# A two-layer trunk on one core: which adaLN vectors TensorE makes around the norms, and which VectorE makes as rows

## The chip, the cores and the metric

The kernel runs on one core of a Trainium2 chip. The metric is the device time of one execution in microseconds (us); lower is better. The core has TensorE (PE; the load of its weights is listed apart as PEld), VectorE (DVE), ScalarE (ACT), GpSimd (POOL) and a queue for transfers (SP), each with its own stream of instructions, which wait for each other by semaphores.

## What is computed

Two layers, each a token mixer and a channel mixer (FFN), on x of 256 tokens by 1024 channels. Each layer first makes six vectors of 1024 from the condition c (adaLN), and each norm is scaled and shifted by two of them:

```python
c_act = jax.nn.silu(c)
for l in range(DEPTH):
    mod = c_act @ w_mod[l] + b_mod[l]
    sh1, sc1, g1, sh2, sc2, g2 = jnp.split(mod, 6, axis=-1)
    h = modulate(rms_norm(x, mix_norm_g[l]), sh1, sc1)
    y = token_mixer(h, ...)          # latent attention, block attention, gated convolution, w_out
    x = x + g1[:, None, :] * y
    h = modulate(rms_norm(x, ffn_norm_g[l]), sh2, sc2)
    x = x + g2[:, None, :] * channel_mixer(h, ...)   # w_up, depthwise conv, silu(a) * b, w_down
```

`modulate(n, sh, sc)` is n * (1 + sc) + sh. So a norm's scale (sc1, sc2) is wanted as soon as that norm's statistics are there; the shift at the same time; the gates g1 and g2 at the end of the mixer and of the FFN.

## The kernel before

x stays on the chip, transposed: eight tiles of 128 channels by 256 tokens. Every matrix is streamed from memory in units of 512 KB. Each matmul is exact to fp32 by three passes: a unit is loaded (line 193), ACT rounds it to a high part `whi` (line 210), DVE takes the difference `wlo` (line 212), and PE multiplies high by high (line 287), low by high (288) and high by low (290); lines 281 to 283 are the same three for a whole flush. All units go through one queue in the order in which the code asks for them.

An adaLN vector of layer l, number r (0 to 5 for sh1, sc1, g1, sh2, sc2, g2), lies in `mod[l]` as eight columns of 128. There are two ways to make one. As **rows** (`mod_row`, lines 369 to 373): for each k of eight a unit of the transposed matrix is loaded (`in_wmr`), DVE multiplies it by silu(c), which stands in every partition (`crow`), and sums along the row (line 367), and adds the bias (368); PE has no share in it. As a **PE part** (`mod_part`, lines 375 to 398): for each k a unit of `in_wm` is loaded and four matmuls with silu(c) as weights take it (line 384); after eight such steps ACT copies the sum (389), PE turns it by two transposes (392), and DVE adds the bias (394). A part is a generator: whoever calls `step` decides where its steps fall in the program.

Before, the twelve vectors are made so: as rows (0,0) and (0,1) in front of the first norm, (0,3) and (0,4) in layer 0's mixer, (1,0) and (1,1) in layer 0's FFN (`rows_left`), (1,2) in layer 1's mixer; as PE parts (0,2) in layer 0's mixer, (0,5) around layer 0's second norm, (1,3) around layer 1's first, (1,4) in layer 1's mixer (among its attention), (1,5) around layer 1's second norm.

A norm inside the program is `norm_stats(fill)`. First two steps (F1) of the part `fill` are taken. Squares (ACT line 475, DVE 483) are summed over channels by PE (487), DVE and POOL make the reciprocal root (465, 466), PE spreads it over the partitions (495), and the other six steps follow the statistics. Then `norm_tile` makes each of the eight tiles: DVE multiplies x by gain and root (528), ACT makes the high part (529), DVE the low one (530). The gain (1 + sc) * g comes from `mod_gain` (536). The part that ran here feeds a vector that is used later; its copy and transposes are taken after the second block of FFN matmuls (`step(fill)` at j == 1), or after the first matmuls of the mixer.

The work in the mixers is put in order by a planner (`STEPS`, `_order`), and a list scheduler then sets the order on each engine; what the code writes late may so stand early on its engine. The lines that the change touches are those of `mod_part`, `norm_stats` and `layer`.

Of the kernel before, what the change touches and what calls it, by code (L numbers as in the profile page):

```python
# [9 lines left out]
F32 = mybir.dt.float32  # L10
# [7 lines left out]
P = 128  # L18
S = 256
NB = 2  # L20
# [14 lines left out]
PB = 4  # L35
DVN = ()
MAHEAD = 0
F1 = 2
MARK = 1
CROWB = 1  # L40
C0K = {}
# [3 lines left out]
HOLD = 0  # L45
SQ4 = 1
CHAIN = 1
RPARTS = [(0, 3), (0, 4), (1, 2)]
RFROM = ("G", 5, 0)
RTO = ("PR", 5)  # L50
MFROM = ("QKV", 2, 0)
# [4 lines left out]
LEAD = 16  # L56
TAILP = 2
FLEAD = 1
ROWS = [(0, 0), (0, 1), (1, 0), (1, 1)] + RPARTS


PARTS = [[(0, r) for r in (2, 3, 4) if (0, r) not in RPARTS], [(1, 4)]]


UNITS = {"KL": 0.65, "QKV": 1, "UQ": 2, "UK": 2, "MA": 0.6, "BA": 0.7, "C": 1, "G": 1, "O": 1, "OC": 0.5, "PR": 1}
# [82 lines left out]
def trunk_kernel(ctx, tc, xT, crow, ccol, pos, invf, modb_d, cols_d, grow_d, wmr, wm, win1, wqkv,  # L148
# [223 lines left out]

        return use_row(wload_row(l, r, k, tag), row, l, r, k, scale)

    def mod_part(l, r, spare=True):

        acc = psa()
        raws = []
        for k in range(KD):
            for i in range(len(raws), min(KD, k + 1 + MAHEAD)):  # L380
                raws.append(wload(wm[l, r, i], SPARE[i % 4], 1) if spare else wload(wm[l, r, i]))
            raw = raws[k]
            for c in range(4):
                te.matmul(acc[32 * c:32 * c + 32, 0:S], cact[:, k:k + 1].to_broadcast([P, 32]),  # L384
                          raw[:, c * S:(c + 1) * S], start=(k == 0), stop=(k == KD - 1),
                          tile_position=(0, 32 * c))
            yield
        g = e1()
        ac.activation(g, acc[:, 0:S], AF.Copy)
        pt = psa()  # L390
        for q in range(2):
            te.transpose(pt[:, q * P:(q + 1) * P], g[:, q * P:(q + 1) * P], ident)
        view = pt[:, 0:S].rearrange("p (q c m) -> p c q m", q=2, c=4)[:, :, :, 0]
        ve.tensor_tensor(mod[l][:, r * 8:r * 8 + 8].rearrange("p (c q) -> p c q", c=4), view,
                         modb[:, l, r * 8:r * 8 + 8].rearrange("p (c q) -> p c q", c=4),
                         op=ALU.add)
        yield
# [5 lines left out]
    def step(gen, n=1):  # L403
        for _ in range(n):
            next(gen, None)
# [257 lines left out]
    def layer(l):  # L663

        sh1 = mod[l][:, 0:8]
        fill = mod_part(1, 3) if l == 1 else None
        hh, hl = new_h()
        if l == 0:

            bc = first_stats(crow0[1])  # L670
            xn = [mq().rearrange("p (k t) -> p k t", k=4) for _ in range(2)]

            bcs = e1()
            ac.activation(bcs, bc, AF.Copy)
            for k in range(KD):
                (gp if XNP and k else ve).tensor_tensor(xn[k // 4][:, k % 4, :], x[:, k, :], bcs, op=ALU.mult)
            mods0, gains = [], []

            def prepare_tile(k):
                raws0 = [wload_row(0, r, k) for r in range(2)]  # L680
                if k == 0:
                    load_rest()
                accs = small(2, "m0", 4)
                for r in range(2):
                    ve.scalar_tensor_tensor(raws0[r], raws0[r], 1.0, crow0[0], op0=ALU.mult, op1=ALU.mult,
                                            accum_out=accs[:, r:r + 1])
                mods0.append(ve.tensor_tensor(mod[0][:, 0:16].rearrange("p (r k) -> p k r", r=2)[:, k, :], accs,
                                              modb[:, 0, 0:16].rearrange("p (r k) -> p k r", r=2)[:, k, :], op=ALU.add))
                g = small(1, "gs", 12)
                i = ve.scalar_tensor_tensor(g, mod[0][:, 8 + k:9 + k], 1.0, cv(l, "mix_g")[:, k:k + 1],  # L690
                                            op0=ALU.add, op1=ALU.mult)
                gains.append(g)
                if HOLD:
                    hold[0] = i.ins

            prepare_tile(0)
        else:
            bc = norm_stats(fill)
        if l == 1:
            gs1 = mod_gain(l, 1, "mix_g")  # L700

        def rows(pp, w, k, b, start, stop):
# [48 lines left out]
        for k in range(KD):  # L751
            if l > 0:
                norm_tile(k, bc, gs1[:, k:k + 1], sh1[:, k:k + 1], hh, hl)
                conv_in(k)
                continue
            t = e1()
            ac.activation(t, xn[k // 4][:, k % 4, :], AF.Identity, scale=gains[k], bias=sh1[:, k:k + 1])
            ac.activation(hh[:, k, :], t, AF.Copy)  # L758
            last = ve.tensor_tensor(hl[:, k, :], t, hh[:, k, :].bitcast(F32), op=ALU.subtract)
            if HOLD > 1:  # L760
                hold[0] = last.ins
            latents(k)
            if k + 1 < KD:
                prepare_tile(k + 1)
            else:
                with tc.issue_after(mods0[-1].ins):
                    make_trig()
            conv_in(k)
            if k in C0K:
                gate_c(0, C0K[k], 3, psa)  # L770
            hold[0] = None
        step(fill or iter(()))
        ahead[0] = AHEAD
        mods = mod_parts(*((*p, False) for p in PARTS[l]))

        if l == 0:
            make_bases()
# [47 lines left out]


        qks = [None, None]
        vb = wk.tile([P, NB, 512], F32, tag="vb", name=nm("vb"), bufs=1)

        pqkv = {}  # L830

# [166 lines left out]

        def conv(j, t0, t1):
            if not cacc:  # L1000
                cacc.append(wk.tile([P, 4, S], F32, tag="lh2", name=nm("cacc"), bufs=1))
            aj = cacc[0][:, j, :]
            for t in range(t0, t1):
                if t == 0:
                    ve.tensor_scalar(aj, upad[:, j, 0:S], cw[:, j * 31:j * 31 + 1], cv(l, "cdw_b")[:, j:j + 1],
                                     op0=ALU.mult, op1=ALU.add)
                else:
                    ve.scalar_tensor_tensor(aj, upad[:, j, t:t + S], cw[:, j * 31 + t:j * 31 + t + 1], aj,  # L1008
                                            op0=ALU.mult, op1=ALU.add)
# [130 lines left out]
                                    x[:, n, :], op0=ALU.mult, op1=ALU.add)  # L1140


        gs2 = mod_gain(l, 4, "ffn_g")
        fill = mod_part(l, 5)
        bc = norm_stats(fill)
        hh, hl = new_h()
        marks = [norm_tile(k, bc, gs2[:, k:k + 1], mod[l][:, 24 + k:25 + k], hh, hl) for k in range(KD)]
        fw = wk.tile([P, 3, 44], F32, tag="fw", name=nm("fw"), bufs=1)
# [6 lines left out]
            ve.tensor_scalar(fb[:, NF:44], cv(l, "fdw_b")[:, NF:44], 0.5, None, op0=ALU.mult)  # L1155
        acc2 = []
        acts = []
        rows_left = [(1, r, k) for r in range(2) for k in range(KD)] if l == 0 else []

        def down(j):  # L1160
            if not acc2:
# [6 lines left out]
                flush(j == NF - 1)  # L1168

        hi_tags[:] = [("whi", 4), ("mq", 3)]  # L1170
        lo_tags[:] = [("wlo", 4), ("qkT", 2), ("wlo", 4), ("kv", 2)] if l else [("wlo", 4), ("qkT", 2), ("wlo", 4), ("kv", 2), ("wlo", 4), ("qkT", 2), ("wlo", 4), ("thc", 1)]
        def up(j):
            pp = psb()
            for _ in range(2):
# [29 lines left out]
        for is_up, j in FFN:  # L1204
            if not is_up:
                down(j)
                continue
            with ExitStack() as es:
                if j < 2:
                    for i in marks[MARK]:  # L1210
                        es.enter_context(tc.issue_after(i.ins))
                up(j)
            if j == 1:
                step(fill)
        hi_tags[:] = [("whi", 4)]
        lo_tags[:] = [("wlo", 4)]
        for n in range(KD):
# [92 lines left out]
```

## Time and profile before

| | |
|---|---|
| median of 3 runs | 938.41 us (935.89 to 938.76) |
| profiled execution | 933.22 us, of which span 931.3 us |
| mean granted clock of PE | 0.983 |
| PE busy | 897.1 us (96%) |
| DVE busy | 793.5 us (85%) |
| ACT busy | 554.0 us (59%) |
| POOL busy | 45.8 us (5%) |
| DMA | 201.59 MB, mean 216 GB/s |
| loads of rows / of PE parts | 56 / 40, 512 KB each |

Busy times count the time in which an engine has work in it. PE's records overlap, and its ends are modelled, so a PE busy in 100% of a stretch can still be faster or slower there: how many matmuls it took says that. A timeline row may join several instructions of one kind (xcount). A number in brackets behind a row is the time in which the engine stood before it, with what released it. In the rows an fp32 matmul of the parts and of the statistics has two records.

### The profile page before, as it was taken

How to read it: one execution, taken by the hardware profiler on the slowest of the kernel's cores; microseconds unless marked ns; L12 is line 12 of the kernel's file. 1: busy time of each engine (PE TensorE's matmuls, PEld its weight loads, DVE VectorE, ACT ScalarE, POOL GpSimd, SP SyncE). 2: the span in 40 equal slices, each digit the busy share in tenths (PEclk: the TensorE clock that was granted, in tenths of full speed). 3: DMA queues.
4: the chain of work that ended last, by engine and by line, in shares of the span. 5: the costliest groups of instructions: out<-in, count | busy, mean ns of one | idle time of the engine just before them, and what ended most of it. 6: DMA issues, size and time to landing. Idle time of an engine off the chain costs nothing.

```text
span 931.3 us, 18548 instructions
## 1 busy us (share of the span) xinstructions
PE 897.1 (96%) x7262; PEld 844.8 (91%) x7262; DVE 793.5 (85%) x1540; ACT 554.0 (59%) x979; POOL 45.8 (5%) x32
## 2 busy tenths in 40 slices
PE   3999999999989999999999999999999999999997
PEld 3998878998987999999979987889999799999997
DVE  5999899999987999988865999999787788777774
ACT  4577688744645655566643775895475566555551
POOL 1011500000000000000000042000000000000000
PEclk7999999999999999999999999999999999999999
DMA  7956524497886888877644565547657677555641
GB/s 282 397 206 209 178 92 155 158 325 274 298 307 234 290 273 286 304 239 224 214 137 129 184 231 184 195 130 270 230 180 259 211 234 223 186 184 187 187 127 46
DMA packets 58264, 201.59 MB, mean 216 GB/s; under 512 B 6976, under 2 KB 8512, under 8 KB 58176
## 3 DMA queue, kind: packets, MB, share of 16 engines
q1 hardware_dynamic: 58176, 200.41, 64.0%
q8 instruction: 57, 0.93, 0.4%
q14 instruction: 31, 0.25, 0.1%
HBM read 199.33 MB, written 1.05 MB: 215 GB/s over the span
## 4 chain that ended last, share of the span: by engine, by line
PE 80%; DVE 10%; DMA 4%; issue 2%; ACT 2%; POOL 2%; SPq 0%; POOLq 0%; DVEq 0%; ACTq 0%
PE psb L287 16%; PE psb L288 15%; PE psb L290 15%; PE psa L287 8%; PE psa L288 8%; PE psa L290 8%; DVE wlo L212 3%; DMA raw<-in_wmr 3%; DVE cacc L1008 2%; PE psa L384 2%; POOL rs L466 2%; PE psa L621 1%; DVE raw L367 1%; PE psa L281 1%; PE psa L633 1%
## 5 line engine op out<-in xcount | busy, mean ns | idle before, releaser
L210 ACT ACTIVATE whi<-raw 128x1024 fp32r<-128x1024 f32 (+2 forms) x286 | 294.6, 1038 | 212.1 <-PE psb L288 101.6
L212 DVE TENSOR_TENSOR wlo<-raw,whi 128x1024 fp32r<-128x1024 f32 (+2 forms) x286 | 340.5, 1195 | 74.0 <-ACT whi L210 62.7
L287 PE MATMUL psb<-hh,whi 128*128 128x256 f32 x1088 | 263.0, 282 | 1.6 <-ACT thc L729 1.2
L288 PE MATMUL psb<-hl,whi 128*128 128x256 f32 x1088 | 260.8, 280 | 0.0
L287 PEld LDWEIGHTS psb<-hh,whi 128*128 128x128 f32 x1088 | 205.0, 189 | 8.6 <-issue 5.3
L288 PEld LDWEIGHTS psb<-hl,whi 128*128 128x128 f32 x1088 | 205.3, 189 | 1.1 <-DVE e L528 0.4
L290 PE MATMUL psb<-hh,wlo 128*128 128x256 f32 x1088 | 149.8, 279 | 0.0
L290 PEld LDWEIGHTS psb<-hh,wlo 128*128 128x128 f32 x1088 | 136.1, 188 | 0.8 <-issue 0.8
L1008 DVE SCALAR_TENSOR_TENSOR cacc<-upad,cw,cacc 128x256 f32<-128x256 f32 x240 | 105.5, 477 | 0.1
L287 PE MATMUL psa<-mhl,whi 128*128 128x256 f32 x400 | 94.9, 279 | 0.1
L288 PE MATMUL psa<-mhl,whi 128*128 128x256 f32 x400 | 94.7, 279 | 0.0
L1187 DVE SCALAR_TENSOR_TENSOR e<-psb,fw,e 128x255 f32<-128x255 f32 (+1 forms) x176 | 83.8, 477 | 8.9 <-ACT e L1185 7.8
L466 POOL TENSOR_TENSOR rs<-rs,mhalf 128x16 f32<-128x16 f32 (+3 forms) x22 | 44.3, 2022 | 688.7 <-DVE rs L465 687.9
L287 PEld LDWEIGHTS psa<-mhl,whi 128*128 128x128 f32 x400 | 75.2, 189 | 0.3 <-ACT mhl L1089 0.3
L288 PEld LDWEIGHTS psa<-mhl,whi 128*128 128x128 f32 x400 | 75.1, 188 | 0.0
L1185 ACT ACTIVATE e<-psb,fb,fw 128x256 f32<-128x256 f32 x88 | 48.5, 551 | 25.8 <-DVE e L1187 14.1
L290 PE MATMUL psa<-mhl,wlo 128*128 128x256 f32 x400 | 54.4, 279 | 0.0
L367 DVE SCALAR_TENSOR_TENSOR raw<-raw,crow 128x1024 f32<-128x1024 f32 x40 | 48.7, 1218 | 5.8 <-DMA raw<-in_wmr 5.8
L290 PEld LDWEIGHTS psa<-mhl,wlo 128*128 128x128 f32 x400 | 49.9, 189 | 0.0
L287 PE MATMUL psb<-whi,hh 128*128 128x416 f32 (+1 forms) x96 | 31.6, 352 | 7.6 <-ACT hh L758 7.6
L1195 ACT ACTIVATE mhl<-e 128x256 fp32r<-128x256 f32 x44 | 18.3, 417 | 27.0 <-DVE e L1193 26.2
L287 PE MATMUL psa<-hh,whi 128*128 128x256 f32 x128 | 30.8, 285 | 0.0
(266 smaller groups left out, 1480.2 us busy)
## 6 DMA issues: line engine op xcount, KB each, us to landing
raw<-in_wup SPq DMA_DIRECT2D x88, 512.0 KB, 4.6
raw<-in_wmr SPq DMA_DIRECT2D x56, 512.0 KB, 5.0
raw<-in_wdn SPq DMA_DIRECT2D x44, 512.0 KB, 4.4
raw<-in_wm SPq DMA_DIRECT2D x40, 512.0 KB, 4.5
raw<-in_wgab SPq DMA_DIRECT2D x32, 512.0 KB, 5.1
raw<-in_wqkv SPq DMA_DIRECT2D x24, 512.0 KB, 4.7
raw<-in_win SPq DMA_DIRECT2D x16, 512.0 KB, 4.7
raw<-in_wgc SPq DMA_DIRECT2D x16, 512.0 KB, 4.0
```

The lines of the kernel that those rows point to most:

```text
L210: ac.activation(hi, raw, AF.Copy)
L212: ve.tensor_tensor(lo, raw, hi.bitcast(F32), op=ALU.subtract)
L287: te.matmul(o, p1[0], p1[1], start=start, stop=False)
L288: te.matmul(o, p2[0], p2[1], start=False, stop=False)
L290: te.matmul(o, p3[0], p3[1], start=False, stop=stop)
L367: ve.scalar_tensor_tensor(raw, raw, scale, row, op0=ALU.mult, op1=ALU.mult, accum_out=acc)
L384: te.matmul(acc[32 * c:32 * c + 32, 0:S], cact[:, k:k + 1].to_broadcast([P, 32]), raw[:, c * S:(c + 1) * S], start=(k == 0), stop=(k == KD ...
L466: gp.tensor_tensor(r, r, mhalf[:, :n], op=ALU.pow)
L1008: ve.scalar_tensor_tensor(aj, upad[:, j, t:t + S], cw[:, j * 31 + t:j * 31 + t + 1], aj, op0=ALU.mult, op1=ALU.add)
L1185: ac.activation(t, src, AF.Identity, scale=fw[:, 2, c:c + 1], bias=fb[:, c:c + 1])
L1187: ve.scalar_tensor_tensor(t[:, d:S], src[:, 0:S - d], fw[:, 2 - d, c:c + 1], t[:, d:S], op0=ALU.mult, op1=ALU.add)
L1195: ac.activation(mh, th, AF.Copy)
```

## The change

Each PE part around a norm becomes the scale that this very norm needs: (0,4) at layer 0's second norm, (1,1) at layer 1's first, (1,4) at layer 1's second. `mod_gain` moves behind the part, F1 goes from two to six, and six buffers are named for the part's loads in front of the norm. The vectors that these parts made become rows: (0,5) in layer 0's FFN, (1,3) written among the first matmuls of layer 1's mixer, (1,5) in layer 1's FFN. The part in layer 1's mixer goes (its vector is now made at the norm), and layer 0's mixer has one vector less as rows. In all 64 loads of rows and 32 of PE parts.

```diff
-F1 = 2
+F1 = 6
-RPARTS = [(0, 3), (0, 4), (1, 2)]
+RPARTS = [(0, 3), (1, 2)]
-ROWS = [(0, 0), (0, 1), (1, 0), (1, 1)] + RPARTS
-PARTS = [[(0, r) for r in (2, 3, 4) if (0, r) not in RPARTS], [(1, 4)]]
+ROWS = [(0, 0), (0, 1), (0, 5), (1, 0), (1, 3), (1, 5)] + RPARTS
+PARTS = [[(0, 2)], []]
...
-    def mod_part(l, r, spare=True):
+    def mod_part(l, r, tags=()):
...
-                raws.append(wload(wm[l, r, i], SPARE[i % 4], 1) if spare else wload(wm[l, r, i]))
+                raws.append(wload(wm[l, r, i], tags[i % len(tags)], 1) if tags else wload(wm[l, r, i]))
...
-        fill = mod_part(1, 3) if l == 1 else None
...
         else:
+            fill = mod_part(l, 1, ("oah", "obh", "vb", "lh0", "lh1", "lh2"))
             bc = norm_stats(fill)
-        if l == 1:
+            step(fill)
             gs1 = mod_gain(l, 1, "mix_g")
...
                 conv_in(k)
+                mod_row(crow1[0], l, 3, k, scale=0.5 if CDMA else 1.0)
                 continue
...
-        step(fill or iter(()))
         ahead[0] = AHEAD
-        mods = mod_parts(*((*p, False) for p in PARTS[l]))
+        mods = mod_parts(*PARTS[l])
...
+        fill = mod_part(l, 4, SPARE + ("vb", "lh2"))
+        bc = norm_stats(fill)
+        step(fill)
         gs2 = mod_gain(l, 4, "ffn_g")
-        fill = mod_part(l, 5)
-        bc = norm_stats(fill)
...
-        rows_left = [(1, r, k) for r in range(2) for k in range(KD)] if l == 0 else []
+        rows_left = [(*p, k) for p in (((0, 5), (1, 0)) if l == 0 else ((1, 5),)) for k in range(KD)]
...
-        lo_tags[:] = [("wlo", 4), ("qkT", 2), ("wlo", 4), ("kv", 2)] if l else [("wlo", 4), ("qkT", 2), ("wlo", 4), ("kv", 2), ("wlo", 4), ("qkT", 2), ("wlo", 4), ("thc", 1)]
+        lo_tags[:] = [("wlo", 4), ("qkT", 2), ("wlo", 4), ("kv", 2), ("wlo", 4), ("qkT", 2), ("wlo", 4), ("thc", 1)]
...
-            if j == 1:
-                step(fill)
```

Two work tiles (`vb` and `cacc`) also get an alignment, so that a load may use their room. How the change moves instructions is shown at three places. The first is PE at layer 0's second norm, before (`raw` is a unit of the part, 487 the statistics, 495 the spreading of the root, 287 and 288 the FFN's first matmuls):

```order
L384 MATMUL psa_3465<-raw_3466,cact 32x256 x4
L384 MATMUL psa_3465<-raw_3472,cact 32x256 x4
L487 MATMUL psb_3478<-ones,e_626_3479 128x1 x2
L487 MATMUL psb_3478<-ones,e_628_3486 128x1 x2
L487 MATMUL psb_3478<-ones,e_630_3493 128x1 x2
L487 MATMUL psb_3478<-ones,e_632_3500 128x1 x2
L384 MATMUL psa_3465<-raw_3513,cact 32x256
L495 MATMUL psb_3510<-ident,rs_3507 128x128 x2
L384 MATMUL psa_3465<-raw_3513,cact 32x256 x3
L384 MATMUL psa_3465<-raw_3519,cact 32x256 x4
L384 MATMUL psa_3465<-raw_3525,cact 32x256 x4
L287 MATMUL psb_3589<-hh_3549,whi_3305 128x256
```

and after (392 are the transposes):

```order
L384 MATMUL psa_3423<-raw_3448,cact 32x256 x4
L384 MATMUL psa_3423<-raw_3454,cact 32x256 x4
L487 MATMUL psb_3460<-ones,e_613_3461 128x1 x2
L487 MATMUL psb_3460<-ones,e_615_3468 128x1 x2
L487 MATMUL psb_3460<-ones,e_617_3475 128x1 x2
L487 MATMUL psb_3460<-ones,e_619_3482 128x1 x2
L495 MATMUL psb_3492<-ident,rs_3489 128x128 x2
L384 MATMUL psa_3423<-raw_3495,cact 32x256 x4
L384 MATMUL psa_3423<-raw_3501,cact 32x256 x4
L392 MATMUL psa_3509<-ident,e_625_3507 128x128 x2
L287 MATMUL psb_3555<-hh_3515,whi_3275 128x256
L287 MATMUL psb_3631<-hh_3515,whi_3356 128x256
```

All eight steps and the transposes now stand ahead of the FFN's first matmul, and six of the steps ahead of the statistics. The second place is PE in layer 1's attention, before (989 are transposes of queries and keys, 564 and 566 the scores):

```order
L989 MATMUL psa_7089<-ident,ma_6710 96x128 x4
L989 MATMUL psa_7095<-ident,ma_7032 96x128 x4
L384 MATMUL psa_7101<-raw_7102,cact 32x256 x4
L989 MATMUL psa_7109<-ident,ma_6687 96x128 x4
L989 MATMUL psa_7115<-ident,ma_6972 96x128 x4
L989 MATMUL psa_7121<-ident,ma_6710 96x128 x4
L989 MATMUL psa_7127<-ident,ma_7032 96x128 x4
L384 MATMUL psa_7101<-raw_7157,cact 32x256
L564 MATMUL psa_7137<-qkT_7076 128x128 x2
L566 MATMUL psa_7139<-qkT_7076 128x256 x2
L566 MATMUL psa_7138<-qkT_7076 128x256
```

and after:

```order
L989 MATMUL psa_7095<-ident,ma_7032 96x128 x4
L989 MATMUL psa_7102<-ident,ma_6687 96x128 x4
L989 MATMUL psa_7108<-ident,ma_6972 96x128 x4
L989 MATMUL psa_7114<-ident,ma_6710 96x128 x4
L989 MATMUL psa_7120<-ident,ma_7032 96x128 x4
L564 MATMUL psa_7130<-qkT_7076 128x128
L566 MATMUL psa_7132<-qkT_7076 128x256
L564 MATMUL psa_7130<-qkT_7076 128x128
L566 MATMUL psa_7132<-qkT_7076 128x256
```

The steps of line 384 no longer stand among the scores. The third place is DVE at the end of the rows in layer 0's FFN (1187, in the changed kernel 1188, is the FFN's convolution; `mod_99` is layer 1's vectors), before:

```order
L1187 SCALAR_TENSOR_TENSOR e_838_4807<-psb_4742,fw_3583,e_838_4807 128x255
L1192 SCALAR_TENSOR_TENSOR e_839_4811<-e_839_4811,e_837_4803 128x256
L1187 SCALAR_TENSOR_TENSOR e_838_4807<-psb_4742,fw_3583,e_838_4807 128x254
L368 TENSOR_TENSOR mod_99<-m_922_5375,modb 128x1
L367 SCALAR_TENSOR_TENSOR raw_5484,m_938_5486<-raw_5484,crow_2206 128x1024
L1193 TENSOR_TENSOR e_839_4811<-e_839_4811,e_838_4807 128x256
L212 TENSOR_TENSOR wlo_4968<-raw_4965,whi_4967 128x1024
L1196 TENSOR_TENSOR mhl_4815<-e_839_4811,mhl_4815 128x256
L368 TENSOR_TENSOR mod_99<-m_938_5486,modb 128x1
L536 SCALAR_TENSOR_TENSOR gs_6127<-mod_99,col_4246 128x8
```

and after (`raw_6133` is the first unit of (1,3)):

```order
L1193 SCALAR_TENSOR_TENSOR e_839_4882<-e_839_4882,e_837_4874 128x256
L1188 SCALAR_TENSOR_TENSOR e_838_4878<-psb_4813,fw_3549,e_838_4878 128x254
L367 SCALAR_TENSOR_TENSOR raw_6133,m_1025_6135<-raw_6133,crow_2206 128x1024
L1194 TENSOR_TENSOR e_839_4882<-e_839_4882,e_838_4878 128x256
L212 TENSOR_TENSOR wlo_5119<-raw_5116,whi_5118 128x1024
L1197 TENSOR_TENSOR mhl_4886<-e_839_4882,mhl_4886 128x256
L368 TENSOR_TENSOR mod_99<-m_1025_6135,modb 128x1
L367 SCALAR_TENSOR_TENSOR raw_6172,m_1031_6174<-raw_6172,crow_2206 128x1024
L1188 SCALAR_TENSOR_TENSOR e_853_4985<-psb_4924,fw_3549,e_853_4985 128x255
L212 TENSOR_TENSOR wlo_5069<-raw_5066,whi_5068 128x1024
L1188 SCALAR_TENSOR_TENSOR e_853_4985<-psb_4924,fw_3549,e_853_4985 128x254
```

Before, the last row is followed by the gain of layer 1's first norm; after, the eight rows of (1,3) follow in the same place.

## Rows read from the trace of the kernel before

**Rows 1.** FFN stretches: us, engines' busy us (x records), PEclk, DMA share, GB/s.

```profile
310.00:460.00 150.00, 150.00 (x1326) 150.00 (x1325) 137.06 (x242) 88.53 (x133) 0.00 (x0) 1.00 0.79 262
744.00:754.00 10.00, 10.00 (x90) 10.00 (x90) 9.02 (x14) 6.09 (x10) 0.00 (x0) 1.00 0.80 277
760.00:910.00 150.00, 150.00 (x1276) 150.00 (x1275) 115.88 (x182) 87.09 (x128) 0.00 (x0) 1.00 0.58 182
```

**Rows 2.** The same view, parts of the two mixers.

```profile
188.00:275.00 87.00, 81.86 (x699) 78.43 (x697) 82.95 (x168) 45.31 (x67) 0.77 (x1) 1.00 0.87 303
275.00:282.00 7.00, 6.63 (x42) 6.54 (x42) 4.63 (x10) 2.56 (x6) 0.00 (x0) 0.76 0.41 147
560.00:600.00 40.00, 38.93 (x312) 31.39 (x311) 36.83 (x78) 29.00 (x76) 5.88 (x2) 1.00 0.56 186
620.00:725.00 105.00, 103.71 (x900) 102.95 (x899) 85.53 (x144) 63.44 (x107) 0.77 (x1) 1.00 0.71 237
```

**Rows 3.** Chain of waits, 188 to 282 us: shares by line.

```profile
by line: DMA raw<-in_wmr 21.5%; DVE wlo L212 19.3%; DVE raw L367 10.2%; issue 7.7%; DVE cacc L1008 5.8%; PE psb L290 3.9%; DVE b L1068 3.2%; PE psa L281 2.5%; PE psa L282 2.4%; PE psb L288 2.1%; PE psa L283 2.1%; PE psb L287 2.1%; DVE e L10
```

**Rows 4.** Timeline 270 to 276: start, us, engine, line, out<-in, xcount [idle <-releaser].

```profile
270.57 1.22 DVE L367 SCALAR_TENSOR_TENSOR raw<-raw,crow 128x1024 f32<-128x1024 f32 x1 [1.82 <-DMA raw<-in_wmr]
273.10 0.39 PE L281 MATMUL psa<-mhl,whi 128*128 128x256 f32 x1 [2.07 <-ACT mhl L1089]
```

**Rows 5.** Rows of adaLN, lines 367 and 368: ns min/median/max.

```profile
L367 DVE SCALAR_TENSOR_TENSOR raw<-raw,crow x40: 1203/1218/1227, 191.2 to 657.7; 128x1024 f32<-128x1024 f32 x40
...
L368 DVE TENSOR_TENSOR mod<-m,modb x40: 142/152/158, 195.2 to 660.0; 128x1 f32<-128x1 f32 x40
```

**Rows 6.** Timeline of layer 1's second norm.

```profile
730.57 1.07 PE L384 MATMUL psa<-raw,cact 128*32 128x256 f32 x16
731.57 1.05 PE L487 MATMUL psb<-ones,e 128*128 128x1 f32 x8
733.07 1.05 PE L487 MATMUL psb<-ones,e 128*128 128x1 f32 x8 [0.45 <-DVE e L483]
735.99 1.26 DVE L528 SCALAR_TENSOR_TENSOR e<-x,gs,psb 128x256 f32<-128x256 f32 x3 [1.67 <-PE psb L495]
737.74 0.64 PE L384 MATMUL psa<-raw,cact 128*32 128x256 f32 x8
738.31 0.39 PE L288 MATMUL psb<-hl,whi 128*128 128x256 f32 x1
```

**Rows 7.** Timeline of PE where that part's transposes stand.

```profile
755.11 0.44 PE L392 MATMUL psa<-ident,e 128*128 128x128 f32 x2
```

**Rows 8.** Chain of waits in layer 1's attention, 560 to 600 us: by line.

```profile
by line: DVE cacc L1008 16.3%; POOL rs L466 14.7%; PE psb L287 8.4%; PE psb L288 7.5%; PE psb L290 7.2%; PE psa L384 7.0%; PE psa L621 6.9%; ACT p L600 6.3%; PE psa L566 5.0%; PE psa L633 3.7%; DVE mx L578 3.0%; DVE mx L581 3.0%; DVE wlo L2
```

**Rows 9.** Lines 389, 536 (ns min/median/max) and loads of in_wm.

```profile
L389 ACT ACTIVATE e<-psa x5: 371/376/384, 253.3 to 754.7; 128x256 f32<-128x256 f32 x5
...
L536 DVE SCALAR_TENSOR_TENSOR gs<-mod,col x3: 160/160/168, 274.3 to 626.3; 128x8 f32<-128x8 f32 x3
...
DMA to landing us min/median/max: 3.4/4.5/7.7
```

**Rows 10.** Timeline of PE, layer 0's second norm.

```profile
282.05 1.07 PE L384 MATMUL psa<-raw,cact 128*32 128x256 f32 x16
291.13 0.39 PE L288 MATMUL psb<-hl,whi 128*128 128x256 f32 x1
```

**Rows 11.** Timeline of PE, layer 1's first norm.

```profile
473.26 1.07 PE L384 MATMUL psa<-raw,cact 128*32 128x256 f32 x16
480.97 0.74 PE L287 MATMUL psa<-hh,whi 128*128 128x256 f32 x4
```

**Rows 12.** PE's busy time and granted clock in the three norms.

```profile
286.00:289.00 3.00, 2.65 (x18) 0.50 0.72 283
477.00:480.00 3.00, 2.53 (x20) 0.52 0.38 152
734.00:737.00 3.00, 2.43 (x30) 1.00 0.91 352
```

More of the change, by code (lines that the diff above doesn't have):

```diff
@@ L827, in layer @@
         qks = [None, None]
-        vb = wk.tile([P, NB, 512], F32, tag="vb", name=nm("vb"), bufs=1)
+        vb = wk.tile([P, NB, 512], F32, tag="vb", name=nm("vb"), bufs=1, align_bytes=LINE)
         pqkv = {}
@@ L1000, in conv @@
             if not cacc:
-                cacc.append(wk.tile([P, 4, S], F32, tag="lh2", name=nm("cacc"), bufs=1))
+                cacc.append(wk.tile([P, 4, S], F32, tag="lh2", name=nm("cacc"), bufs=1, align_bytes=LINE))
             aj = cacc[0][:, j, :]
```

## Prediction

> **What bounds the kernel now.** I read the busy times by stage first, then the chains of waits in the two stages that are not full, then the timelines around the three norms that have a PE part in them. The stretches of 150 us in the two FFNs [rows 1] show PE full at full clock; the other stages [rows 2] show three places where it is not. The end of layer 0's mixer (188 to 275) has 87.00 - 81.86 = 5.14 us of idle PE, and VectorE is busy 82.95 of 87 with the DMA engines at 0.87. The next 7 us lose 0.37 us more and run at a mean clock of 0.76. Layer 1's attention (560 to 600) leaves 1.07 us idle, with VectorE at 36.83 of 40. In the first of them the chain of waits names the rows of adaLN: their loads hold 21.5% of it and their multiply 10.2% [rows 3]. The last of these rows shows how that reaches PE: VectorE waits 1.82 us for the load, multiplies from 270.57, and the projection's first matmul on PE has then stood 2.07 us at 273.10 [rows 4]. So a stage in which PE is full pays for PE work alone; the stage with rows pays for VectorE and for loads.
>
> All sums below are made against the profiled execution, 933.22 us (span 931.3 and 1.92 outside it). That run is 5.19 us under the median of the runs, 938.41; I carry the difference over to the median unchanged.
>
> **Term 1: eight rows leave layer 0's mixer.** A row costs VectorE 1.218 + 0.152 = 1.37 us [rows 5], eight of them 11.0 us. PE can gain only what it loses there: 5.14 + 0.37 idle and 7.00 x 0.24 = 1.7 us of clock, together 7.2. Layer 1's same stage has eight rows already and still 1.29 us idle [rows 2], so some 5.9 are within reach. Against that, the eight rows that stay still wait for loads, and two loads more for the norm's part now go out before the norm. I take -5; bounds -7.2 and -2.5 (half of the idle stays), and zero if the loads alone set the pace.
>
> **Term 2: the PE part in layer 1's mixer goes.** A step is four matmuls, which the profile lists as eight records (each of these fp32 matmuls stands there twice). Sixteen records, two steps, fill the 1.00 us from 730.57 to 731.57 [rows 6], so a step is 0.50 and eight are 4.0; with the two transposes (0.44 [rows 7]) it is 4.4 us of PE, and the ACT copy and VectorE addition go too. In the attention stage, where the steps stand, the chain of waits gives them 7.0% of 40 us = 2.8 [rows 8]; the rest stood in waits on softmax and on VectorE (16.3% of the chain is the convolution's accumulate). I take -2.8; bounds -4.4 and 0, if VectorE, 92% busy there, is simply late next.
>
> **Term 3: the scale becomes part of the path, at three norms.** Before, the part in a norm fed something used much later, so its steps filled PE while statistics ran, and its last steps and transposes fell among the next matmuls. Now the sum of squares waits for six steps, and the norm's first tile waits for the eighth step, the copy, the transposes, the addition and the gain. From the first step, by layer 1's second norm [rows 6]: six steps 3.0, the statistics' sixteen records 2 x 1.05 = 2.1 (ends at 5.1; the wait of 0.45 inside goes), then 735.99 - 734.12 = 1.87 for rstd, power and broadcast. Steps seven and eight stand behind the broadcast, 1.0, then copy 0.38, transposes 0.44, addition (as the gain) 0.16, gain 0.16 [rows 7, 9], and four hand-overs of some 0.07, a guess from the gaps between these rows. The first tile then starts at 9.4 instead of 735.99 - 730.57 = 5.4. The dense stretch of matmuls came 738.31 - 735.99 = 2.3 us behind the first tile, with one late step in it (737.74 to 738.31); without that step it is 1.8, and dense matmuls start at 11.2 us. Before, the dense stretch starts at 738.31 - 730.57 = 7.7, and two steps (0.57 each) and the transposes (0.44) come later: 9.3 in all. The same reading gives 291.13 - 282.05 = 9.1 + 1.14 + 0.44 = 10.7 at layer 0's second norm [rows 10] and 480.97 - 473.26 = 7.7 + 3 x 0.57 + 0.44 = 9.9 at layer 1's first [rows 11]. At full clock the three cost 1.9 + 0.5 + 1.3 = +3.7. But the chain there is longer in its thin stretch, and two of the three norms already run it at half clock: 0.50, 0.52, against 1.00 at the third [rows 12]. Where half clock stays, the way to the dense stretch is longer by what layer 0's norm shows over layer 1's second, 9.1 - 7.7 = 1.4; for two norms that makes +6.5, which I take. Bounds: +3.7 and +11 (all three at half clock, and the last loads late).
>
> The Trainium skill, "TensorE: Matmul & The Clock Gate", section "HAM oscillation — how this bites in real kernels", says that a PE left idle between bursts falls back to half clock and starts the next burst cold. By it the third norm would fall too, which makes term 3 +7.9 and the whole 1.4 worse; the trace agrees at two norms and not at the third, so I keep two.
>
> **The loads of the part.** Six of the eight now have a buffer of their own in front of the norm; the last two go out when steps one and two have been read, about 0.9 us in, and are wanted at 6.9. A load of this kind lands after 4.5 us at the median and 7.7 at most [rows 9]. So usually nothing, at worst 7.7 - 6.0 = 1.7 per norm: that is in the bound of term 3.
>
> **Term 4: rows land in layer 0's FFN.** The code writes the eight rows of layer 1's g1 among layer 1's first matmuls, but VectorE's order has them ahead of that, at the end of layer 0's FFN, so 24 rows stand there in place of 16. VectorE is busy 137.06 of 150 us there [rows 1]: 13 of room, and 11.0 come in. It fits, at about 99%. I take +0.5; bounds 0 and +4, as the operand split of each weight unit shares that engine. In layer 1's FFN eight rows meet VectorE at 115.88 of 150 [rows 1], room for 34: nothing; bytes are the same, eight loads less and eight more.
>
> **Term 5: the pitch of matmuls.** In two stretches of 150 us with PE full, at the same granted clock, layer 0's FFN has 1326 matmuls and layer 1's 1276 [rows 1]: 113.1 against 117.6 ns each. The slow stretch starts at two transposes put into the stream (755.11 [rows 7]); before them, from 744 to 754, 90 matmuls touch 10 us [rows 1], some two of them over an edge: 113.6 apart. After the change no transposes are in the stream of either FFN: they come ahead of it. If the slow pitch comes with them, some 1390 matmuls from there to the end of layer 1's FFN (164 us at 117.6 ns) win 4.5 ns each, -6.2. I take it, as the nearest thing that the trace shows at the switch. Bounds: -6.2, 0 (the pitch has another cause), and +6.2 if layer 0's FFN falls into it instead.
>
> [...]
>
> **Sum.** -5 - 2.8 + 6.5 + 0.5 - 6.2 = -7.0: 926.2 for an execution like the profiled one, 931.4 from the median.
>
> **Rivals.**
> A pitch that stays: term 5 is zero, everything else as above, -0.8: 937.6. For it: nothing in the order of waits explains the pitch, and matmuls in layer 1's mixer show the slow one as well. Against: the switch sits exactly at the transposes.
> Slower, by the scale's chain: all three norms at half clock and the last two loads late, term 3 = +11, pitch not gained: -5 - 2.8 + 11 + 0.5 = +3.7, 942.1. Place: between the end of a projection and the next matmuls. It decides once the three norms cost over 10 us together. For it: two norms at half clock now, the loads' spread to 7.7. Against: layer 1's second norm keeps full clock.
> The change does not do what it says: rows meant to stand around layer 1's first norm crowd layer 0's FFN, and VectorE becomes the bound there, term 4 = +4: -3.5, 934.9. For it: 137.06 of 150 busy with 16 rows. Against: the 13 us of room.
> More relief: term 1 = -7, term 2 = -4.4, term 3 = +3.7, term 4 = 0, term 5 = -6.2: -13.9, 924.5.
>
> **How the numbers follow.** Under 0.3% (2.8 us) a measurement of this kernel can't be told from no change; faster is below 935.6, slower above 941.2. Chances: forecast 0.42 (own range 926 to 935), pitch that stays 0.23, slower chain 0.15, VectorE bound 0.08, more relief 0.12. Faster: 0.42 + 0.12, most of the VectorE case (0.05) and a little of the first rival (0.03): 0.62. Slower: 0.15 and 0.03 from the first and third rivals' upper ends: 0.18. Same: the rest, 0.20. The range reaches from the middle of the relief case and the forecast's bounds, 922, to the first rival's upper end, 941; that leaves out most of the slower case and the far end of the relief one.
>
> **What would show it.** In the new profile: the row multiplies of layer 0's mixer 8 instead of 16, with PE idle under 2 us between 188 and the projection (term 1); no adaLN matmuls in layer 1's attention (2); the first tile of each norm 9.4 us behind the first step at full clock, and what clock is granted there (3); VectorE at 97% or more in layer 0's FFN, with PE still full (4); matmuls per 150 us in both FFNs, 1326 or 1276 (5). I am wrong if PE waits for VectorE in layer 0's FFN, if the norms take over 14 us each, or if layer 1's FFN still shows 117.6 ns.

## The result: slower by 0.7%

Over 20 runs the changed kernel takes 941.40 us at the median (936.44 to 949.45); 20 runs of the kernel before take 938.26 (930.55 to 946.08). The ratio is 1.0071, with a 95% interval of 1.0047 to 1.0094: 938.26 x 0.0071 = +6.7 us, where -7.0 was forecast. The ratio is taken over executions in the faster of two states alone; the medians, taken over all, lie 3.1 us apart. The profiled execution took 941.92 us, with a span of 939.6.

Both kernels issue the same 6264 exact matmuls (lines 281 to 283 and 287 to 290) in almost the same order (106 places hold one of another line or shape), so the time between the starts of the n-th and the m-th of them can be compared across kernels, stage by stage. Single executions differ, so the table gives all profiles of this study that have a stage in the one form or the other (us; in brackets the number of profiles and their range).

| stage (exact matmuls) | as before | as changed | difference | forecast |
|---|---|---|---|---|
| end of layer 0's mixer (1450 to 1547) | 15.3 (5: 13.6 to 16.6) | 11.6 (11: 11.5 to 11.7) | -3.7 | term 1: -5 |
| layer 1's attention (3550 to 3760) | 63.3 (7: 62.6 to 64.5) | 63.8 (7: 61.2 to 65.6) | +0.5 | term 2: -2.8 |
| three norms (1547 to 1640, 3131 to 3240, 4679 to 4850) | 73.3 (5: 72.6 to 74.9) | 82.2 (6: 80.7 to 85.5) | +8.9 | term 3: +6.5 |
| layer 0's FFN (1640 to 3131) | 171.6 (8: 169.5 to 176.3) | 176.7 (7: 173.6 to 178.4) | +5.1 | term 4: +0.5 |
| layer 1's FFN (4850 to 6150) | 153.1 (4 of 4) | 147.3 (10 of 11) | -5.8 | term 5: -6.2 |

For the last row the form is whether transposes stand in the stream behind its second block. Left out are kernels made to change a stage in another way, with one exception: the 173.6 us of layer 0's FFN are of after_tr, in whose stream transposes were inserted. Without it the changed form has 177.2 there and the difference is +5.6. The differences of the table sum to +5.0, inside the interval of 4.4 to 8.8 that the ratio gives.

### The profile page after: what moved, and what is told of

Read it like the earlier page. It is cut to its first block, busy times and chain, and to the rows that moved or that the text cites. A ratio compares the mean times of both kernels' runs of the same rounds, so it can differ in the third digit from the quotient of the medians.

```text
span 939.6 us, 18397 instructions
## 1 busy us (share of the span) xinstructions
PE 895.8 (95%) x7196; PEld 850.6 (91%) x7196; DVE 800.3 (85%) x1563; ACT 553.4 (59%) x978; POOL 53.1 (6%) x32
## 4 chain that ended last, share of the span: by engine, by line
PE 85%; DVE 7%; ACT 2%; POOL 2%; DMA 2%; issue 2%; SPq 0%; POOLq 0%; DVEq 0%; ACTq 0%
PE psb L287 17%; PE psb L288 17%; PE psb L290 16%; PE psa L287 8%; PE psa L288 8%; PE psa L290 8%; DVE cacc L1008 2%; POOL rs L466 2%; PE psa L384 2%; DVE wlo L212 2%; PE psa L621 1%; PE psa L566 1%; PE psa L281 1%; PE psa L633 1%; PE psa L283 1%
## 5 line engine op out<-in xcount | busy, mean ns | idle before, releaser
L287 PE MATMUL psb<-hh,whi 128*128 128x256 f32 x1088 | 266.4, 285 | 6.1 <-ACT hh L529 3.0
L288 PE MATMUL psb<-hl,whi 128*128 128x256 f32 x1088 | 265.3, 284 | 0.3
L287 PEld LDWEIGHTS psb<-hh,whi 128*128 128x128 f32 x1088 | 208.1, 192 | 10.8 <-ACT hh L529 3.5
L288 PEld LDWEIGHTS psb<-hl,whi 128*128 128x128 f32 x1088 | 208.6, 192 | 0.9 <-DVE hl L530 0.7
L287 PE MATMUL psa<-mhl,whi 128*128 128x256 f32 x400 | 95.2, 279 | 0.0
L466 POOL TENSOR_TENSOR rs<-rs,mhalf 128x16 f32<-128x16 f32 (+3 forms) x22 | 51.6, 2354 | 693.9 <-DVE rs L465 680.3
L367 DVE SCALAR_TENSOR_TENSOR raw<-raw,crow 128x1024 f32<-128x1024 f32 x48 | 58.4, 1217 | 2.9 <-DMA raw<-in_wmr 2.9
L290 PE MATMUL psa<-mhl,wlo 128*128 128x256 f32 x400 | 54.6, 279 | 0.0
```

The source lines that it names most:

```text
L287: te.matmul(o, p1[0], p1[1], start=start, stop=False)
L288: te.matmul(o, p2[0], p2[1], start=False, stop=False)
L290: te.matmul(o, p3[0], p3[1], start=False, stop=stop)
L367: ve.scalar_tensor_tensor(raw, raw, scale, row, op0=ALU.mult, op1=ALU.mult, accum_out=acc)
L466: gp.tensor_tensor(r, r, mhalf[:, :n], op=ALU.pow)
```

## The profile after

Busy time in the stages that answer to [rows 1, 2] (us, busy us of PE, PEld, DVE, ACT, POOL, clock, DMA share, GB/s):

```profile
190.00:275.00 85.00, 81.67 (x688) 78.53 (x687) 73.39 (x140) 43.99 (x65) 0.78 (x1) 1.00 0.78 267
275.00:282.00 7.00, 6.96 (x58) 6.64 (x56) 5.96 (x14) 3.72 (x7) 0.00 (x0) 1.00 0.83 309
310.00:460.00 150.00, 150.00 (x1276) 150.00 (x1275) 139.60 (x258) 84.73 (x127) 0.00 (x0) 1.00 0.80 266
574.00:614.00 40.00, 35.12 (x278) 31.75 (x276) 34.19 (x75) 28.15 (x76) 5.03 (x2) 0.91 0.22 74
770.00:920.00 150.00, 150.00 (x1326) 150.00 (x1325) 129.32 (x218) 89.46 (x135) 0.00 (x0) 1.00 0.66 211
```

The last 7 us of layer 0's mixer are full and at full clock now (0.76 in [rows 2]). The two FFNs have changed places: layer 0's has the 1276 matmuls in 150 us that layer 1's had, and layer 1's the 1326. Layer 1's attention has lost PE time: 35.12 of 40 us busy at a clock of 0.91, against 38.93 at 1.00.

The timeline of layer 1's second norm, the answer to [rows 6]:

```profile
741.97 2.80 PE L384 MATMUL psa<-raw,cact 128*32 128x256 f32 x48
744.70 1.95 PE L487 MATMUL psb<-ones,e 128*128 128x1 f32 x16
747.76 1.22 PE L495 MATMUL psb<-ident,rs 128*128 128x128 f32 x4 [1.12 <-POOL rs L466]
748.91 1.94 PE L384 MATMUL psa<-raw,cact 128*32 128x256 f32 x16
750.97 0.38 ACT L389 ACTIVATE e<-psa 128x256 f32<-128x256 f32 x1 [7.50 <-PE psa L384]
751.41 0.44 PE L392 MATMUL psa<-ident,e 128*128 128x128 f32 x2 [0.56 <-ACT e L389]
752.28 1.27 DVE L528 SCALAR_TENSOR_TENSOR e<-x,gs,psb 128x256 f32<-128x256 f32 x3
753.36 0.51 PE L287 MATMUL psb<-hh,whi 128*128 128x256 f32 x2 [1.52 <-ACT hh L529]
```

PE stands three times: 1.12 us for POOL's root, 0.56 for the copy, 1.52 for the first tile. The first tile starts 10.31 us behind the first step (9.4 was worked out for full clock); at layer 0's norm it was 8.94, at layer 1's first 9.61. The granted clock (behind the count of records) falls at all three, also at the one that kept it in [rows 12]:

```profile
294.00:296.00 2.00, 2.00 (x11) 0.50 0.91 334
488.00:490.00 2.00, 1.46 (x14) 0.50 0.00 1
748.00:750.00 2.00, 2.00 (x16) 0.50 0.84 328
```

## The experiments

**Both kernels once more**, for another profile each.

> The kernel before once more, for one profile. Theory (drawn pitch): the pitch of the FFNs' matmuls (113.3 or 117.8 ns) is drawn anew in each execution when the stream restarts; then the pair (layer 0, layer 1) need not be (113.3, 117.8) again, and a stretch that differs moves the span by 6.4 us. Rival (the place of the transposes sets it): the pair is (113.3, 117.8) again.

> The changed kernel once more, for one profile. Drawn pitch: the pair need not be (117.8, 113.3) again. Rival (the change sets it): (117.8, 113.3) again. By the matmul counts the three norms should again cost 6 to 8 us over before, whatever the pitch; a rival that their cost was a chance of one execution would show them within 2 us of before.

The kernel before now had 117.8 ns in both FFNs (layer 0's FFN 176.3 us, where the first profile had 169.9), and its span was 939.7. So the pitch of layer 0's FFN is no property of the kernel. The changed one showed (117.8, 113.3) again, and its norms again cost 82.8 us against 73.3 and 74.9.

```profile
320.00:470.00 150.00, 150.00 (x1275) 150.00 (x1275) 131.51 (x231) 85.52 (x127) 0.00 (x0) 1.00 0.77 248
770.00:920.00 150.00, 150.00 (x1276) 150.00 (x1275) 115.79 (x184) 84.58 (x125) 0.00 (x0) 1.00 0.58 179
```

**Each layer's half alone.** half0 is the kernel before with layer 0's edits, half1 with layer 1's:

```diff
# half0, in short: 24 rows in layer 0's FFN, two for one block where they would not fit
+rows_left = [(*p, k) for p in ((0, 5), (1, 0), (1, 1)) for k in range(KD)] if l == 0 else []
+fill = mod_part(0, 4, ...); bc = norm_stats(fill, 6); step(fill); gs2 = mod_gain(0, 4, "ffn_g")
# half1, one line of it: layer 0's mixer and second norm as before, layer 1 as changed
+RPARTS = [(0, 3), (0, 4), (1, 2)]
```

> Layer 0's half of the change alone: (0,4) as the part at layer 0's second norm with six steps ahead of the statistics, eight rows fewer in layer 0's mixer, 24 rows in layer 0's FFN; layer 1 as before. Theory (layer 1 loses): layer 0's relief of some 4.5 us is worth more than the 1.6 us that its norm costs, so some -3 us against before, ratio 0.997. Rival (24 rows on VectorE make layer 0's FFN late): +1 to +4 us, with PE idle in that FFN.

> Layer 1's half alone: (1,1) and (1,4) as parts at layer 1's norms, no part in its attention, (1,3) and (1,5) as rows; layer 0's mixer and second norm as before. Theory (layer 1 loses): +1.8 and +3.7 us at the two norms and +1 to +2 in the attention, so +6 to +8 us against before, ratio 1.007 to 1.009, with half clock in the attention. Rival (the loss is layer 0's): within 2 us of before.

half0: ratio 1.0065 (1.0028 to 1.0103), the rival, at some +6 us by the ratio where it named +1 to +4. Layer 0's FFN took 183.5 us in the profile, the slowest of half0's twelve executions (949.75 us, median 941.98), and PE, busy 20.00 of 20 us from 440 to 460, was busy 15.82 of 20 us at the end (460 to 480) with VectorE at 18.32. Its 24 rows are not placed as in the change, so its size is not the change's. half1: 1.0046 (1.0009 to 1.0083), less than expected, but the stages lose where the theory had it: norms of layer 1 +3.6 and +3.9 over the first profile of before, attention 65.6 with 10.2 us at half clock, and layer 1's FFN 5.8 shorter.

**A part back in layer 1's attention**, and **fewer steps ahead of the statistics**:

```diff
# after_m5: the changed kernel, (1,5) as a part there and no rows in layer 1's FFN
-PARTS = [[(0, 2)], []]
+PARTS = [[(0, 2)], [(1, 5)]]
# after_f1_2: the changed kernel
-F1 = 6
+F1 = 2
```

> The changed kernel with a PE part back in layer 1's attention: (1,5) is made there and not as rows in layer 1's FFN. Theory (the part's steps kept the clock up): the attention stage (from the 3550th to the 3760th exact matmul) falls from 64.8 to 65.6 us back to 62.6 to 64.4 and shows 3.4 us or less at half clock instead of 10.2; in all -2 us against the changed kernel. Rival (the forecast's term 2: the steps stand on the path): the stage grows by 2.8 us to about 68.

> The changed kernel with two steps of the part ahead of the statistics instead of six, so that four or more fall into the wait for POOL. Theory (the norms' length is the chain of steps and waits in it): each of the three norms some 1 us shorter, less half clock there, -2 to -4 us against the changed kernel. Rival (the last loads decide, as they are wanted earlier): norms as long as now, PE waiting for loads of in_wm.

after_m5: 1.0054 (1.0023 to 1.0085), not clear of the changed kernel. Half clock fell to 3.4 us as the theory said, but the stage took 66.3: neither account holds alone. after_f1_2: 1.0043 (1.0009 to 1.0077), no clear gain and neither account; layer 0's norm took 22.2 us (23.1 to 24.9 in the changed form), layer 1's 27.4 and 34.8 (24.4 to 26.7 and 33.0 to 33.8), and PE waited for no load of in_wm. The attention, without a part and with 3.4 us at half clock, took 61.5. What both showed was not expected: layer 0's FFN at the fast pitch, and still 176.1 and 178.4 us long. Of after_m5, PE (idle time in brackets) and two stretches:

```profile
466.51 0.39 PE L281 MATMUL psa<-mhl,whi 128*128 128x256 f32 x1 [1.61 <-ACT mhl L1196]
467.53 0.38 PE L282 MATMUL psa<-mhl,whi 128*128 128x256 f32 x1 [0.64 <-DVE mhl L1197]
472.78 0.62 PE L281 MATMUL psa<-mhl,whi 128*128 128x256 f32 x3 [2.38 <-ACT mhl L1196]
```

```profile
310.00:460.00 150.00, 150.00 (x1326) 150.00 (x1326) 139.76 (x257) 84.27 (x126) 0.00 (x0) 1.00 0.81 267
465.00:470.00 5.00, 2.86 (x22) 2.66 (x23) 4.93 (x9) 3.62 (x6) 0.00 (x0) 1.00 0.79 256
```

PE runs fast until 465 and then stands 4.63 us for the last blocks' activations, while VectorE is busy 4.93 of 5 us; half clock follows (3.4 us).

**The eight rows that landed in layer 0's FFN left out.** In after_no13 (1,3) isn't made, and layer 1's second norm uses layer 0's shift; the eight loads go with the rows.

```diff
-                mod_row(crow1[0], l, 3, k, scale=0.5 if CDMA else 1.0)
```

> The changed kernel without the eight rows of (1,3) (layer 1's second norm uses layer 0's shift instead), so that layer 0's FFN has 16 rows. Theory (24 rows make VectorE the bound of layer 0's FFN whenever PE runs at the fast pitch): layer 0's FFN (1640th to 3131st exact matmul) 170 us at 113.3 ns, 176 at 117.8, with no wait for VectorE at its end; on the mean -3 us against the changed kernel. Rival (something else makes the end of that FFN late): 176 us at either pitch, within 1 us of the changed kernel.

Ratio to before 0.998 (0.9946 to 1.0015), so 0.9% below the changed kernel, more than expected; the two intervals do not overlap. Layer 0's FFN took 170.1 us at the fast pitch, with no wait at its end:

```profile
310.00:460.00 150.00, 150.00 (x1326) 150.00 (x1325) 137.73 (x240) 88.64 (x132) 0.00 (x0) 1.00 0.78 250
460.00:465.00 5.00, 4.87 (x43) 4.67 (x41) 4.17 (x9) 2.24 (x4) 0.00 (x0) 1.00 0.77 235
```

**The pitch.** after_tr puts two transposes at several places into the FFNs of the changed kernel; before_trfirst moves the end of the parts ahead of the FFN, before_trlate behind its last block.

```diff
# after_tr
+            if j % 4 == 1:
+                te.transpose(pt[:, q * P:(q + 1) * P], x[:, 0, q * P:(q + 1) * P], ident)   # q = 0, 1
# before_trfirst: step(fill) behind norm_stats(fill) instead of at j == 1
# before_trlate: the copy at j == 1 into a tile of its own, the rest of step(fill) at
-            if j == 1:
+            if j in (1, NF - 1):
```

> The changed kernel with two transposes of resident data, used by nothing, put into both FFNs' matmuls at five places, each in front of some 220 matmuls. Theory (the pitch is drawn at each restart of the stream): the stretches between them show both 113.3 and 117.8 ns, changing at the transposes and nowhere else. Rival (transposes in the stream give 117.8): all stretches behind one at 117.8. Rival (the pitch belongs to a place in the program): layer 0's FFN all at 117.8, layer 1's all at 113.3.

> The kernel before with the copy, transposes and addition of the norms' parts in FFN taken ahead of the FFN's first matmul, as in the changed kernel, and nothing else. The forecast's term 5 (transposes in the stream bring 117.8): layer 1's FFN at 113.3, -6 us. Drawn pitch: either pitch in either FFN, and over the runs no difference beyond 1 to 2 us.

> The kernel before with the transposes and the addition of the norms' parts in the FFNs moved from behind the second block of FFN matmuls to behind the last one (the copy stays where it was); nothing else. Theory (transposes put into layer 1's stream bring 117.8 ns there): layer 1's FFN (4850th to 6150th exact matmul) 147.3 us instead of 153.1, in all -5.8 us and a ratio near 0.994; layer 0's may show either pitch. Rival (the pitch is drawn, transposes or not): 153.1 in layer 1's FFN as often as not, a ratio between 0.997 and 1.000.

after_tr shows both pitches, changing at the inserted transposes in both directions. Its matmuls in five stretches of layer 0's FFN, PE alone:

```profile
296.00:328.00 32.00, 32.00 (x274) 1.00 0.75 250
332.00:362.00 30.00, 30.00 (x267) 1.00 0.80 261
365.00:395.00 30.00, 30.00 (x267) 1.00 0.84 292
398.00:428.00 30.00, 30.00 (x257) 1.00 0.85 278
432.00:462.00 30.00, 30.00 (x267) 1.00 0.68 201
```

30 us hold 267 or 257 records; in layer 1's FFN it was 257 in one of four such stretches. In all profiles together, every change of pitch inside an FFN stands at a place where the next matmul starts 0.25 us or more behind the last. before_trfirst brought layer 1's FFN to 147.3, but lost 0.85% (1.0085, 1.0051 to 1.0119): with four buffers the last loads come late, PE waits for them with nothing else in front of it (1.55 and 1.15 us at layer 1's norm, 2.47 and 2.58 at layer 0's), and the two norms grow by some 7 us each. before_trlate has the gain without that price: ratio 0.9941 (0.9909 to 0.9972), layer 1's FFN 147.3, as expected, although layer 0's was at the slow pitch in its profile:

```profile
315.00:465.00 150.00, 150.00 (x1276) 1.00 0.77 251
760.00:910.00 150.00, 149.93 (x1323) 1.00 0.63 194
```

**Layer 0's relief without the norms**, alone and with before_trlate:

```diff
# before_04m: (0,4) as a second part in layer 0's mixer
-RPARTS = [(0, 3), (0, 4), (1, 2)]
+RPARTS = [(0, 3), (1, 2)]
```

> The kernel before with the eight rows of (0,4) taken out of layer 0's mixer and (0,4) made as a second PE part there; norms and layer 1 as before. Theory (the relief of the mixer's end is worth 3 us by itself and the part's steps fall into PE's waits for POOL): the 1450th to the 1547th matmul 11.6 us instead of 13.6 to 16.6, the attention no longer than 50 us, ratio 0.996 to 0.998. Rival (the part's 4.4 us of PE stand on the path): 3 us won, 4 lost, ratio 1.000 to 1.002.

> Both of these edits together. Theory: they act in different stages and add, -8 us, ratio about 0.991. Rival (either gives nothing): 0.994 to 1.000.

before_04m: 0.9994 (0.9954 to 1.0033): the mixer's end took 11.7 us as expected, but the stage with layer 0's attention (450 to 600) took 50.6, not the 50 or less of the theory, and 54.6 with both edits, where kernels with layer 0's mixer as before have 48.6 to 51.6; the ratio doesn't tell the theory from the rival. Both edits: 0.9917 (0.9887 to 0.9948), median 928.86 us, the best kernel here, as expected; that it beats before_trlate alone isn't shown, since the intervals overlap.

**The gain's wait and the part's PE work.** after_offpath is the changed kernel with the gains made from layer 0's sc1; after_warm the changed kernel with a part's matmuls on resident data in layer 1's attention, their sum unused.

```diff
# after_offpath
-            gs1 = mod_gain(l, 1, "mix_g")
+            gs1 = mod_gain(l, 1, "mix_g", src=0)
# ... and gs2, behind both second norms, in the same way
# after_warm: at the old places of the part, for each k and c
+                te.matmul(acc[32 * c:32 * c + 32, 0:S], cact[:, k:k + 1].to_broadcast([P, 32]), x[:, k, :], ...)
```

> The changed kernel with the three norms' gains made from layer 0's sc1, which is there long before, so that no norm tile waits for the part; the part is still made at each norm in the same order on PE. Theory (the gain behind the part's end is what the norms pay): each norm 1.5 to 2.5 us shorter, the sum over the three stages 77 to 78 us in place of 82, with 8 or less of half clock in the sum. Rival (PE's steps themselves in that place): within 1 us of the changed kernel.

> The changed kernel with the PE work of a part, but on resident data, without loads, rows or any use of its sum, at the old places in layer 1's attention. Theory (what the steps did there was to keep the clock): the attention stage (3550th to 3760th exact matmul) shows 3.4 us or less at half clock and takes 62 to 63 us, against 65.3 where 10.2 us are at half clock and 61.3 where 3.4 are. Rival (loads and VectorE, not the clock): half clock 10.2 us again and 66 us or more.

after_offpath: ratio to before 0.9988 (0.9944 to 1.0032), and the three norms 73.8 us; 1.6 more came right behind the first (1640 to 1720), so 75.4 in place of 82.2. Of layer 1's second norm:

```profile
735.52 2.80 PE L384 MATMUL psa<-raw,cact 128*32 128x256 f32 x48
742.07 0.87 DVE L528 SCALAR_TENSOR_TENSOR e<-x,gs,psb 128x256 f32<-128x256 f32 x2 [1.67 <-PE psb L495]
743.99 0.50 PE L287 MATMUL psb<-hh,whi 128*128 128x256 f32 x2
```

The first tile starts 6.55 us behind the first step, and PE has no wait left in front of line 287. So it is the gain's wait that the norms pay for, not the steps' place on PE: of the 8.9 us of the table 2.1 stay. after_warm, a single run, decides nothing: the scheduler moved other work into the stage as well (77.1 us, and 68.8 for the next 540 matmuls, against 73.4 in the profile of the change), PE still stood 3.94 and 3.33 us, and 13.7 us ran at half clock. In that run PE work at those places didn't keep the clock; what would is open.

## Why the prediction was wrong

**The step that failed first is term 4**: "It fits, at about 99%. I take +0.5". It costs +5.1 in the stage, and leaving the eight rows out takes 0.9% off the whole. The sum was of averages: 13 us of room in a stretch of 150. But the rows don't spread over that room. VectorE's row multiplies (line 367) in stretches of 20 us, busy us and records, two for a row, of before:

```profile
360.00:380.00 20.00, 6.12 (x10) 1.00 0.89 303
400.00:420.00 20.00, 0.00 (x0) 1.00 0.71 229
```

and of after_m5, whose FFN starts at the same time (303.1 us) and runs at the same pitch:

```profile
340.00:360.00 20.00, 2.45 (x4) 1.00 0.77 266
380.00:400.00 20.00, 5.84 (x10) 1.00 0.90 300
400.00:420.00 20.00, 6.12 (x10) 1.00 0.87 304
```

and all of VectorE right behind them:

```profile
420.00:440.00 20.00, 19.75 (x38) 1.00 0.80 258
```

The rows stand no denser than before, five in 20 us at most in either, but they last some 40 us longer: until 130 us behind the start of the FFN's stage, where before they end at 91, so VectorE has too little of the stage left to catch up. By the starts of each block's first activation on ACT (line 1186, in after_no13 1185), the 13th block stands 95.2 us behind the stage's start in after_m5 and 97.9 in after_no13, both at the fast pitch; the 17th, when the rows are done, 129.4 and 125.4; the last 164.2 and 159.4. So the last block is 4.8 us late, and PE stands 4.63 us at the end. The rival had this mechanism, at +4 and with a chance of 0.08. It was rated low because room was read as a mean over the stretch.

At the slow pitch VectorE all but keeps up (175.9 to 177.6 us with 24 rows, where PE waits 0 to 1.59 us; 176.0 to 176.3 with 16); at the fast one PE arrives early and waits (176.1 to 178.4 against 169.5 to 171.2). So with 24 rows that FFN takes 175.9 us or more whatever the pitch, and a fast draw is worth nothing there. In the profile of the change itself, where the prediction meant to see it, PE doesn't wait: it drew the slow pitch, and VectorE was busy 139.60 of 150 us, not 97%. Whether 24 rows make the slow draw more frequent isn't shown (three of six profiles with the changed kernel's rows there, after_tr left out, and two of eight with 16).

**Term 2** was to give -2.8 and gave +0.5. The case of its bound 0, VectorE late next, is part of what happened. PE's longest wait in front of the attention's line 566, of before, of the change and of after_no13:

```profile
581.63 1.99 PE L566 MATMUL psa<-qkT 96*128 96x256 f32 x8 [1.07 <-ACT p L600]
```

```profile
592.41 2.08 PE L566 MATMUL psa<-qkT 96*128 96x256 f32 x4 [4.76 <-DVE cacc L1008]
```

```profile
580.14 2.07 PE L566 MATMUL psa<-qkT 96*128 96x256 f32 x4 [3.18 <-ACT p L600]
```

The steps had stood in a wait for softmax and VectorE; without them the wait is longer. But the seven profiles without the part are of two kinds, and POOL's time goes with them. At the start of the stage its power op on 128x8 took 4.93 or 4.94 us in the four profiles in which the stage took 64.8 to 65.6 us (10.2 of them at half clock), and 1.65 in the three with 61.2 to 62.6 (3.4 to 6.8 at half clock). Of the changed kernel, with VectorE's wait for it:

```profile
558.71 4.94 POOL L466 TENSOR_TENSOR rs<-rs,mhalf 128x8 f32<-128x8 f32 x1 [1.05 <-PE psa L288]
563.68 0.69 DVE L972 TENSOR_TENSOR ma<-kv,rs 128x512 f32<-128x512 f32 x1 [1.53 <-POOL rs L466]
```

and of after_no13:

```profile
548.05 1.65 POOL L466 TENSOR_TENSOR rs<-rs,mhalf 128x8 f32<-128x8 f32 x1 [1.05 <-DVE rs L465]
```

In all seven profiles as before the op took 1.65 us, in after_m5 4.94. Compared like with like, the stage without the part is 1.5 us shorter where the op took 1.65 (61.7 on the mean against 63.3), and 1.0 where it took 4.94 (65.3 against the 66.3 of after_m5, one profile). So the removal wins some 1.0 to 1.5 of the 2.8 us that were read from 7.0% of a chain: reading that share as time that vanishes was the error. The rest of the way to +0.5 goes with POOL's longer op, which no term had. Why it takes longer isn't shown, nor whether the change brings it on: it did in six of nine profiles with layer 1's norms as changed, and in none of the seven as before.

**Term 3** had the right mechanism and was 2.4 us small, inside its bounds. The chain was sized well (9.4 against 8.94, 9.61 and 10.31), but half clock was given to two norms, and all three have it: in the three stages together 3.4 to 6.8 us run at half clock as before and 17.1 to 30.7 as changed. Half clock at the third norm too, 1.4 more by the prediction's own working, would have made it +7.9. PE's idle pieces of 1.1, 0.6 and 1.5 us stand at each of the three norms. The Trainium skill, "TensorE: Matmul & The Clock Gate", section "HAM oscillation — how this bites in real kernels", says that a PE left idle between bursts falls back to half clock; the trace of the changed kernel agrees at all three norms (granted clock 0.50).

**Term 1** gave -3.7 of -5, inside its bounds: the last 7 us are full, but 3.3 us of idle PE stay earlier in the mixer.

**Term 5** held where it was taken: layer 1's FFN, 153.1 us in all four profiles with the transposes in its stream behind the second block, 147.3 in ten of eleven without; after_offpath had 153.1 without any. So the number came, but the cause given for it isn't shown. Its other bound, layer 0's FFN at the slow pitch, came too, in the profiles of the changed kernel; with sixteen rows either pitch is seen with and without transposes. The pitch is set where the stream restarts and stays until the next restart. What sets it there is open. The Trainium skill, "TensorE: Matmul & The Clock Gate", section "Back-to-back issue gap", gives a stream of weight loads and matmuls one sustained spacing per width, about 81 ns for 128 columns and 131 for 512; no long stream here has those widths, and for 256 columns the trace has two at one clock. before_trlate moved the ratio by about the difference.

The forecast's -7.0 and the measured +5.0 of the stages lie 12.0 apart: 4.6 from term 4, 3.3 from term 2, 2.4 from term 3, 1.3 from term 1, 0.4 from term 5.

## What to carry to other kernels

Room on a second engine is worth what it is at the pace of the first and in the stretch where the work lands; ask how long the extra work lasts and what is left to catch up in. Work that stands in a wait is nearly free, and taking it out gives back less than its own time (here 1.0 to 1.5 us of 4.4). When kernels differ in a stage, look first for an instruction there that is alike in both and took another time. Where a stream of equal matmuls runs for 150 us, count them: a pitch set at its start can be worth more than the edit, so compare executions by stages and not by two totals.

## What was not expected of the hardware

- The same matmuls, at a granted clock of 1.00 and with PE full, run at one start in 113.3 or in 117.8 ns, constant over some 1400 of them; in the FFNs it changes only where the stream is broken, and one kernel shows both in different executions. For one FFN that is 6 us.
- POOL's power op on one tile took up to 3.81 us in the profile before and up to 7.84 in that of the change, half0, half1, after_warm and the kernel with both edits, for the same 22 instructions. The stage around it (layer 0's attention, 450 to 600) took 51.6 to 54.6 us in these five and 48.6 to 50.6 in the other eleven. In layer 1's attention another of them took 1.65 or 4.94 us (see term 2). Spans on POOL are rough, and the cause wasn't sought.
